# An attention layer on one core: the norm's reciprocal root made from ScalarE's square root and one Newton step, and parts of stage one placed sooner

## The chip, the cores and the metric

One core of a Trainium2 chip runs the whole program. A core has TensorE (PE, matrix products into PSUM banks), VectorE (DVE), ScalarE (ACT), GpSimd (POOL) and SyncE (SP, which here issues DMAs). Each engine takes its instructions strictly from its own list; engines wait for each other by semaphores. The metric is the device time in microseconds (us) of one execution, as a median of runs.

## What is computed

One layer of a bidirectional encoder on 2048 tokens of width 1024: an RMS norm, one projection to q, k, v and a gate, two-dimensional neighbourhood attention with 16 heads of 64, the gate, an output projection with a residual, and a second norm. What the change touches is the first norm and the projection that follows it:

```python
def rmsnorm(x, g):
    xf = x.astype(jnp.float32)
    y = xf * lax.rsqrt(jnp.mean(xf * xf, axis=-1, keepdims=True) + RMS_EPS)
    return (y * g.astype(jnp.float32)).astype(x.dtype)

def neighbourhood_mixer(h, w_in, rpb):
    B, S, _ = h.shape
    proj = h @ w_in
    q, k, v, gate = jnp.split(proj, 4, axis=-1)
    ...
```

## The kernel before

**Chunks and stages.** The 2048 tokens are four chunks of 512. Stage one projects chunks 0 and 1, stage two part of the work for chunks 2 and 3, and the rest of that is fed between the attention's products. float32 operands are split into a high and a low part (`h`, `l`, or `t` and `f` tiles of type F32R), so a product of 128x512 blocks is three matmuls for each of four blocks: twelve matmuls in a row on PE. Products are combined by a seven-product (Strassen-like) scheme over two chunks and two halves of the weights: `P` from 1 to 7, whose operands are the quarters A of the weights or their sums S1 to S4 (`seven.sum`, on DVE), and the quarters B of the inputs or their sums T1 to T4.

**Names.** `form` splits a weight quarter or sum: ACT makes the high part of `f`, DVE the low part. `split` does the same for inputs and gives the tiles `t`, `h`, `l` and `sixths`; `sums4` makes the T4 sums in `spot` and `land` on DVE. `seven.keep` copies a finished bank to `p1`, `acc` (ACT); `add` makes `u` from a bank and that copy (DVE) before a later product goes on in the same bank; `out_` and `evac`/`first_out` write `tmp` from a bank. `tmp` is multiplied by `rb` (on DVE for the first six units, on POOL from unit 6 on) and stored through DRAM tiles `kd`, `qd`, `sgd`. `keep`, `form` and the gate's tanh all stand in ACT's one list.

**Products.** `seq` in `stage_one` lists the products as pairs (unit n, P); `step(i)` issues product i. Positions 0 to 11 are P = 1 and 2 of units 0 to 5. From 12 on they are (0,6), (1,6), (0,7), (0,5), (1,7), (0,4), (1,5), (0,3), (1,4), (1,3), then the same ten for units 2 and 3: product 14 is (0,7), product 17 is (0,4), product 22 is (2,6) and product 24 is (2,7). P = 6, 7 and 4 of a unit share a bank, so product 14 may start only when DVE has taken `u` of product 12 out of it, and product 24 only after `u` of product 22. All other work is attached to a position, either as code between two `step` calls or by `on(i, f, ...)`, which calls `f` after product i. There is no scheduler behind it: the order in which the code issues instructions is the order on each engine.

**The statistics.** The inputs arrive a second time as rows (`load_rows`). `square_rows` squares eight half rows of a chunk on ACT and accumulates the sums. `stats(c)` turns them into a mean square `m` and a reciprocal root `rt`, 128x4 numbers. For chunk 0 the root is fourteen small DVE steps with `m` and `rth` (half of `rt`, by which the values are scaled); for chunks 1, 2 and 3 DVE makes a first guess and POOL three Newton steps of four instructions each. `diagonal(c)` puts `rt` on diagonals `dg` and splits them into `dgh` and `dgl`; `spread_rstd(c)` multiplies these with ones on PE into `prb`, which gives the row `rb[c]` that every output of the chunk is multiplied with. For chunk 1 this pair of matmuls stands behind product 20. Outputs of chunk 1 that were made before are held and scaled by `scale_held`.

**ACT's tables.** ACT's functions lie in tables; the program loads one at its start and another for the square roots of the last norm.

Of the kernel before, what the change touches and what calls it, by code (L numbers as in the profile page):

```python
# [11 lines left out]
F32 = mybir.dt.float32  # L12
F32R = mybir.dt.float32r
BF16 = mybir.dt.bfloat16
I32 = mybir.dt.int32
AF = mybir.ActivationFunctionType
OP = mybir.AluOpType
# [60 lines left out]
def build(ctx, tc, x, xr, xt, wg, bias, w_out, n0, nf, out):  # L78
    nc = tc.nc
# [12 lines left out]
    def pool(name, bufs):  # L92
        p = ctx.enter_context(tc.tile_pool(name=name, bufs=bufs))
        return lambda shape, dt, nm: p.tile(shape, dt, name=nm, tag=name)
# [28 lines left out]
    ev = pool("ev", 8)  # L123
    rbp = pool("rbp", 3)
    tiny = ctx.enter_context(tc.tile_pool(name="tiny", bufs=6))
# [15 lines left out]
    rt = one.tile([128, 16], F32, name="rt")  # L141
    rth = one.tile([128, 8], F32, name="rth")
# [1 line left out]
    accs = [one.tile([128, 512], F32, name=f"acc{i}") for i in range(2)]  # L144
    nc.scalar.dma_start(g0, n0)

    def rsqrt(y, m, n, by=None):
        h = tiny.tile([128, 8], I32, name="h")[:, :n]
        a = tiny.tile([128, 8], F32, name="a")[:, :n]
        nc.vector.tensor_scalar(h, m.bitcast(I32), 1, None, op0=OP.arith_shift_right)  # L150
        nc.vector.tensor_scalar(y.bitcast(I32), h, -1, 0x5F3759DF, op0=OP.mult, op1=OP.add)
        for _ in range(3):
            if by is None:
                nc.vector.tensor_tensor(a, y, y, OP.mult)
                nc.vector.scalar_tensor_tensor(a, a, -0.5, m, op0=OP.mult, op1=OP.mult)
                nc.vector.scalar_tensor_tensor(y, a, 1.5, y, op0=OP.add, op1=OP.mult)
            else:
                by.tensor_tensor(a, y, y, OP.mult)
                by.tensor_tensor(a, a, m, OP.mult)
                by.tensor_scalar(a, a, -0.5, 1.5, op0=OP.mult, op1=OP.add)  # L160
                by.tensor_tensor(y, y, a, OP.mult)

    hh, hl = {}, {}
    rb = {}
# [45 lines left out]
    def square(t, half, tile_):  # L210
        c = t // 4
        if c not in rows:
            rows[c] = tiny.tile([128, 8], F32, name="ss")
        i = 2 * (t % 4) + half
        nc.scalar.activation(tile_, tile_, AF.Square, accum_out=rows[c][:, i:i + 1])

    def stats(c, by=None):
        ss = rows.pop(c)
        m = tiny.tile([128, 8], F32, name="m")[:, :4]
        nc.vector.tensor_tensor(m, ss[:, 0:8:2], ss[:, 1:8:2], OP.add)  # L220
        nc.vector.tensor_scalar(m, m, 1.0 / D, EPS, op0=OP.mult, op1=OP.add)
        rsqrt(rt[:, 4 * c:4 * c + 4], m, 4, by)
        if c < 2:
            (by or nc.vector).tensor_scalar(rth[:, 4 * c:4 * c + 4], rt[:, 4 * c:4 * c + 4], 0.5, None, op0=OP.mult)

    dgs = {}

# [43 lines left out]
    for n, (k, j, ph, c) in enumerate(halves):  # L271
        a = (KINDS[k] + j, ph)
# [259 lines left out]
    def gain(f, k):  # L532
        r = 4 * (int(f[1]) - 1) + k
        return g0[:, r:r + 1]
# [8 lines left out]
    def split_to(h, l, t, scale):  # L543
        if scale is None:
            nc.scalar.activation(h, t, AF.Copy)
            nc.vector.tensor_tensor(l, t, h.bitcast(F32), OP.subtract)
        else:
            nc.scalar.activation(h, t, AF.Copy, scale=scale)
            nc.vector.scalar_tensor_tensor(l, t, scale, h.bitcast(F32), op0=OP.mult, op1=OP.subtract)
# [27 lines left out]
    def place_of(slot_):  # L577
        return slot_[0]([128, slot_[1]], F32R, "t")[:, :512] if isinstance(slot_, tuple) else slot_
# [39 lines left out]
    def stage_one():  # L618
# [16 lines left out]
        def split(f, t, ks, scale=None):  # L635
            for k in ks:
                if f[0] == "T":
                    X1.setdefault(f, []).append(tuple(place_of(a) for a in slots[f][2 * k:2 * k + 2]))
                split_to(*X1[f][k], land[t][k], gain(scale, k) if isinstance(scale, str) else scale)
# [3 lines left out]
        def load_rows(c, hs, p):  # L643
            for h in hs:
                t, j = 4 * c + h // 2, h % 2
                rows_in[t, j] = p([128, 512], F32, "row")
                nc.sync.dma_start(rows_in[t, j], xr[t * 128:t * 128 + 128, 512 * j:512 * j + 512])

        def square_rows(c, hs):
            for h in hs:  # L650
                t, j = 4 * c + h // 2, h % 2
                square(t, j, rows_in.pop((t, j)))
# [35 lines left out]
        E, C = 6, 42  # L688
# [4 lines left out]
        seven = seven_products(us, 0, X1, None)[2]  # L693
        made = [0]

        def forms(to):
            while made[0] <= min(to, len(seq) - 1):
                seven.form(*seq[made[0]])
                made[0] += 1
# [3 lines left out]
        def on(i, f, *a):  # L703
            todo.setdefault(i, []).append((f, a))
# [3 lines left out]
        def step(i):  # L708
            n, P = seq[i]
            seven.product(n, P)  # L710
            now, then[:] = then[:], []
            if i >= 2 * E:
                seven.after(n, P, then)
            elif P == 1:
                seven.keep(n, kp([128, 960], F32, "p1")[:, :512] if n > 3 else accs[n - 2] if n > 1 else None)
            for f in now:
                f()
            for f, a in todo.pop(i, ()):
                f(*a)
# [20 lines left out]
        def sums4(*ks):  # L740
            for k in ks:
                d = land["x21"][k]
                nc.vector.scalar_tensor_tensor(d, d, gain("x21", k), land["x11"][k], op0=OP.mult, op1=OP.subtract)
# [98 lines left out]
        for n in range(2):  # L842
            for f in ("S1", "S2"):
                seven.sum(n, f)
        split("T2", "x11", (1, 2))
        step(7)
        split("T2", "x11", (3,))
        step(8)
        spread_rstd(0)
        forms(12)  # L850
        step(9)
        square_rows(1, range(4))
        load_rows(1, range(4, 8), ev)
        forms(13)
        split("T3", "x22", (0, 1))
        step(10)
        seven.sum(0, "S3")
        forms(14)
        split("T3", "x22", (2, 3))
        step(11)  # L860
        seven.sum(1, "S3")
        first_out(0)
        first_out(1)
        sums4(0)
        forms(15)
        for k in range(4):
            if k < 3:
                on(12 + k, sums4, k + 1)
            on(12 + k, split, "T4", "x21", (k,))
        on(14, square_rows, 1, range(4, 8))  # L870
        on(15, first_out, 2)
        on(16, first_out, 3)
        on(16, stats, 1, nc.gpsimd)
        on(18, diagonal, 1, ev, True)
        on(20, spread_rstd, 1)
        on(21, seven.scale_held)
        on(14, seven.sum, 0, "S4")
        on(16, seven.sum, 1, "S4")

        def ask_pair(a):  # L880
            spot = mkp([128, 3, 512], F32, "raw")
# [25 lines left out]
        for m in range(8):  # L907
            on(C + 5 * m, ask_rows, m)
            on(C + 5 * m + 4, square_more, m)
            if m % 4 == 3:  # L910
                on(C + 5 * m + 4, stats, 2 + m // 4, nc.gpsimd)
        for j in range(4):
            on(C + 9 * j, value_rows, j)
            for d, f in ((3, "S1"), (4, "S3"), (5, "S2"), (6, "S4")):
# [873 lines left out]
    for m in range(cycles + 1):  # L1788
        a = amount[m] - 8
# [89 lines left out]
```

## Time and profile before

| what | value |
|---|---|
| runs: median (lowest to highest of 3) | 1016.49 us (1015.69 to 1017.59) |
| profiled execution: device time | 1016.97 us |
| its span, first to last instruction | 1015.2 us |
| mean granted clock of PE | 0.996 |
| busy: PE, DVE, ACT, POOL | 998.7, 775.3, 511.6, 155.9 us |
| DMA: mean over the span | 225 GB/s |

The profile is of one execution. Its device time is 1.8 us more than its span, which runs from the first to the last instruction. A line number such as L449 is the line of the kernel that issued the instruction, `out<-in` are tile names without their numbers. In a timeline each row has its start, its length, engine, line, operation, tiles, the number of instructions merged into it, and in brackets the idle time of that engine before it with what ended it. Stage one takes the first quarter of the span.

### The profile page before, as it was taken

To read this page: it belongs to the slowest core of one execution; us is meant where nothing else is said; L and a number is where in the kernel's file an instruction comes from. 1 tells how busy PE (TensorE), PEld (TensorE's weight loads), DVE (VectorE), ACT (ScalarE), POOL (GpSimd) and SP (SyncE) were. 2 spreads that over 40 slices of the span, in tenths; PEclk is the share of its full clock that TensorE was granted. 3 is DMA by queue.
4 is the path that set the end of the run, shared out by engine and by line. 5 is a ranking of instruction groups with operands and counts; after the bars stand their busy time and mean duration, and the time that the engine had idled before them with its cause. 6 is when DMAs were issued, how large, how long until landed. Compare 5 with 4: busy or idle time off the path is not lost. (4 is left out here: it accounts for less than half of the span.)

```text
span 1015.2 us, 19596 instructions
## 1 busy us (share of the span) xinstructions
PE 998.7 (98%) x6904; PEld 797.1 (79%) x6904; DVE 775.3 (76%) x1710; ACT 511.6 (50%) x1257; POOL 155.9 (15%) x263
## 2 busy tenths in 40 slices
PE   9999999999999999999999999999999999999997
PEld 6877888878888888888888777777777767777876
DVE  5988888978665876766765676778788888787876
ACT  7863235445335342333434465677767657553443
POOL 0002001242200000000000123243333323221100
PEclk9999999999999999999999999999999999999999
DMA  8934437767957846656565797879987779799553
GB/s 293 351 101 131 152 123 257 242 218 255 353 174 231 270 121 191 208 185 188 196 203 182 221 272 233 267 232 285 282 253 260 202 242 289 224 347 356 138 157 104
DMA packets 150122, 228.19 MB, mean 225 GB/s; under 512 B 13640, under 2 KB 65096, under 8 KB 150024
## 3 DMA queue, kind: packets, MB, share of 16 engines
q1 hardware_dynamic: 148152, 223.92, 68.8%
q0 software_dynamic: 1440, 2.62, 1.7%
q8 instruction: 54, 0.88, 0.3%
q14 instruction: 44, 0.36, 0.1%
q10 hardware_dynamic: 432, 0.40, 0.1%
HBM read 160.83 MB, written 66.06 MB: 223 GB/s over the span
## 5 line engine op out<-in xcount | busy, mean ns | idle before, releaser
L1314 POOL TENSOR_SCALAR x<-x,st 128x360 f32<-128x360 f32 (+5 forms) x192 | 106.5, 571 | 529.1 <-DVE st L1307 528.8
L449 PE MATMUL pp<-h,f 128*128 128x512 f32 x576 | 186.3, 391 | 0.0
L449 PE MATMUL pp<-t,f 128*128 128x512 f32 x702 | 172.0, 390 | 3.0 <-DVE u L462 3.0
L449 PEld LDWEIGHTS pp<-t,f 128*128 128x128 f32 x702 | 131.5, 188 | 31.4 <-ACT f L431 2.9
L1302 ACT ACTIVATE x<-x,st 128x360 f32<-128x360 f32 (+5 forms) x256 | 134.2, 525 | 26.4 <-DVE st L1296 26.4
L449 PEld LDWEIGHTS pp<-h,f 128*128 128x128 f32 x576 | 108.8, 189 | 22.8
L449 PE MATMUL pp<-l,f 128*128 128x512 f32 x288 | 112.5, 391 | 0.0
L1296 DVE CUSTOM_DVE_ANT_0 x<-s,em 128x360 f32<-128x360 f32 (+5 forms) x256 | 102.4, 454 | 1.8 <-PE s L1287 1.4
L432 DVE TENSOR_TENSOR f<-raw,f 128x512 fp32r<-128x512 f32 x105 | 75.8, 727 | 21.3 <-ACT f L431 21.1
L1361 PEld LDWEIGHTS o<-pta,vt 120*64 120x64 f32 (+2 forms) x1024 | 68.7, 137 | 22.7 <-DVE st L1296 15.2
L1361 PE MATMUL o<-pta,vt 120*64 120x192 f32 (+5 forms) x1024 | 83.4, 316 | 0.3 <-issue 0.3
L431 ACT ACTIVATE f<-raw 128x512 fp32r<-128x512 f32 x105 | 63.2, 621 | 40.7 <-DVE raw L438 25.8
L1331 DVE COPY pta<-ph 120x512 f32<-120x512 f32 (+5 forms) x96 | 56.0, 637 | 32.7 <-PE ph L1342 32.5
L1287 PE MATMUL s<-kt,q 64*64 64x360 f32 (+5 forms) x1024 | 78.7, 420 | 1.2 <-DVE y L1437 1.0
L1333 ACT ACTIVATE pta<-ph 120x512 f32<-120x512 f32 (+5 forms) x96 | 46.8, 558 | 62.4 <-PE ph L1342 62.3
L449 PEld LDWEIGHTS pp<-l,f 128*128 128x128 f32 x288 | 54.4, 189 | 11.4
L1287 PEld LDWEIGHTS s<-kt,q 64*64 64x64 f32 x1024 | 41.5, 131 | 23.1 <-ACT pta L1333 6.1
L613 PE MATMUL pv<-wh,t 128*128 128x512 f32 x176 | 56.1, 389 | 0.0
L449 PE MATMUL pp<-sixths,f 128*128 128x512 f32 x198 | 52.7, 389 | 0.0
L1647 PE MATMUL py<-woh,f 128*128 128x512 f32 x160 | 50.9, 390 | 0.9 <-DVE y L1437 0.9
L1342 PEld LDWEIGHTS ph<-ident,x 64*120 64x120 f32 (+2 forms) x1408 | 42.5, 128 | 11.3 <-issue 9.5
L470 POOL TENSOR_TENSOR tmp<-tmp,rb 128x512 f32<-128x512 f32 x18 | 28.5, 1591 | 143.8 <-DVE tmp L467 117.6
(225 smaller groups left out, 1867.6 us busy)
## 6 DMA issues: line engine op xcount, KB each, us to landing
raw<-in_wg_dram SPq DMA_DIRECT2D x124, 256.0 KB, 5.1
row<-in_xr_dram SPq DMA_DIRECT2D x34, 256.0 KB, 5.8
vd<-v SPq DMA_DIRECT2D x32, 256.0 KB, 3.3
sgd<-sg SPq DMA_DIRECT2D x32, 256.0 KB, 5.6
q<-qd SPq DMA_DIRECT2D x32, 256.0 KB, 5.6
sgt<-sgd SPq DMA_DIRECT2D x32, 256.0 KB, 6.8
ogd<-og SPq DMA_DIRECT2D x32, 256.0 KB, 3.4
kt<-kd SPq DMA_DIRECT2D x16, 480.0 KB, 6.8
```

The costliest lines, as they stand in the source:

```text
L431: nc.scalar.activation(t[:, 0], src, AF.Copy)
L432: nc.vector.tensor_tensor(t[:, 1], src, t[:, 0].bitcast(F32), OP.subtract)
L449: nc.tensor.matmul(B[n, P], t[:, int(m == 2), c], x[k][int(m == 1)], start=P in (1, 6, 5) and k == 0 and m == 0, stop=k == 3 and m == 2, s ...
L613: nc.tensor.matmul(p, a[:, o], b, start=P in (1, 6, 5) and k == 0 and m == 0, stop=k == 3 and m == 2, skip_group_check=True)
L1287: nc.tensor.matmul(pst[s][h * 64:h * 64 + 64], qt[a, g * 64:g * 64 + 64], kt[a, :r1 - r0, c0:c0 + 8 * WIDE[C]].rearrange("p r (s c) -> p s ...
L1296: nc.vector.tensor_tensor_reduce(X[i, C][s], pst[s], EM[p, ROW_TYPE[T]][C > 0][s], -1.0, 1e38, OP.add, OP.min, st[:, o:o + 1])
L1302: nc.scalar.activation(X[i, C][s], X[i, C][s], AF.Exp, bias=st[:, o:o + 1], scale=-1.0, accum_out=st[:, 4 + o:5 + o])
L1314: nc.gpsimd.tensor_scalar(X[i, C][s], X[i, C][s], st[:, o:o + 1], 1.0, op0=OP.mult, op1=OP.mult)
L1331: nc.vector.tensor_copy(o, i_)
L1333: nc.scalar.activation(o, i_, AF.Copy)
L1361: nc.tensor.matmul(o[s * 64:s * 64 + 64, g0 * 64:g1 * 64], vt[:k, strip, s * 64:s * 64 + 64], t[:k, n * 64:(n + g1 - g0) * 64], start=stri ...
L1647: nc.tensor.matmul(B[m, P], t[:, a, c], b, start=P in (1, 6, 5) and k == 0 and i == 0, stop=k == 3 and i == 2, skip_group_check=True)
```

## The change

`rsqrt` takes a new form for all four chunks: ACT's square root of `m`, DVE's reciprocal, and one Newton step of three DVE instructions. The halving `rth` for chunk 0 goes from DVE to POOL. In `stage_one` the four row squares 0 to 3 of chunk 1 move from behind product 9 to behind product 7, squares 4 to 7 from 14 to 12, and the loads of rows 4 to 7 go with the former; the S3 sums of units 0 and 1 move from products 10 and 11 to 7, the splits of T3 one product ahead, the T4 sums of blocks 1 to 3 one product ahead, the `first_out` of unit 2 from 15 to 14; statistics, diagonal and spreading of chunk 1 move from products 16, 18 and 20 to 13, 15 and 17, and `scale_held` from 21 to 18.

```diff
--- before.py
+++ after.py
@@ -144,21 +144,13 @@
     accs = [one.tile([128, 512], F32, name=f"acc{i}") for i in range(2)]
     nc.scalar.dma_start(g0, n0)
 
-    def rsqrt(y, m, n, by=None):
-        h = tiny.tile([128, 8], I32, name="h")[:, :n]
-        a = tiny.tile([128, 8], F32, name="a")[:, :n]
-        nc.vector.tensor_scalar(h, m.bitcast(I32), 1, None, op0=OP.arith_shift_right)
-        nc.vector.tensor_scalar(y.bitcast(I32), h, -1, 0x5F3759DF, op0=OP.mult, op1=OP.add)
-        for _ in range(3):
-            if by is None:
-                nc.vector.tensor_tensor(a, y, y, OP.mult)
-                nc.vector.scalar_tensor_tensor(a, a, -0.5, m, op0=OP.mult, op1=OP.mult)
-                nc.vector.scalar_tensor_tensor(y, a, 1.5, y, op0=OP.add, op1=OP.mult)
-            else:
-                by.tensor_tensor(a, y, y, OP.mult)
-                by.tensor_tensor(a, a, m, OP.mult)
-                by.tensor_scalar(a, a, -0.5, 1.5, op0=OP.mult, op1=OP.add)
-                by.tensor_tensor(y, y, a, OP.mult)
+    def rsqrt(y, m):
+        a = tiny.tile([128, 8], F32, name="a")[:, :4]
+        nc.scalar.activation(a, m, AF.Sqrt)
+        nc.vector.reciprocal(y, a)
+        nc.vector.tensor_tensor(a, y, y, OP.mult)
+        nc.vector.scalar_tensor_tensor(a, a, -0.5, m, op0=OP.mult, op1=OP.mult)
+        nc.vector.scalar_tensor_tensor(y, a, 1.5, y, op0=OP.add, op1=OP.mult)
 
     hh, hl = {}, {}
     rb = {}
@@ -214,14 +206,14 @@
         i = 2 * (t % 4) + half
         nc.scalar.activation(tile_, tile_, AF.Square, accum_out=rows[c][:, i:i + 1])
 
-    def stats(c, by=None):
+    def stats(c):
         ss = rows.pop(c)
         m = tiny.tile([128, 8], F32, name="m")[:, :4]
         nc.vector.tensor_tensor(m, ss[:, 0:8:2], ss[:, 1:8:2], OP.add)
         nc.vector.tensor_scalar(m, m, 1.0 / D, EPS, op0=OP.mult, op1=OP.add)
-        rsqrt(rt[:, 4 * c:4 * c + 4], m, 4, by)
+        rsqrt(rt[:, 4 * c:4 * c + 4], m)
         if c < 2:
-            (by or nc.vector).tensor_scalar(rth[:, 4 * c:4 * c + 4], rt[:, 4 * c:4 * c + 4], 0.5, None, op0=OP.mult)
+            nc.gpsimd.tensor_scalar(rth[:, 4 * c:4 * c + 4], rt[:, 4 * c:4 * c + 4], 0.5, None, op0=OP.mult)
 
     dgs = {}
 
@@ -843,39 +835,40 @@
             for f in ("S1", "S2"):
                 seven.sum(n, f)
         split("T2", "x11", (1, 2))
+        square_rows(1, range(2))
         step(7)
         split("T2", "x11", (3,))
+        square_rows(1, range(2, 4))
+        load_rows(1, range(4, 8), ev)
+        for n in range(2):
+            seven.sum(n, "S3")
         step(8)
         spread_rstd(0)
         forms(12)
+        split("T3", "x22", (0, 1))
         step(9)
-        square_rows(1, range(4))
-        load_rows(1, range(4, 8), ev)
         forms(13)
-        split("T3", "x22", (0, 1))
+        split("T3", "x22", (2, 3))
         step(10)
-        seven.sum(0, "S3")
-        forms(14)
-        split("T3", "x22", (2, 3))
-        step(11)
-        seven.sum(1, "S3")
         first_out(0)
         first_out(1)
-        sums4(0)
+        forms(14)
+        step(11)
+        sums4(0, 1)
         forms(15)
         for k in range(4):
-            if k < 3:
-                on(12 + k, sums4, k + 1)
+            if k < 2:
+                on(12 + k, sums4, k + 2)
             on(12 + k, split, "T4", "x21", (k,))
-        on(14, square_rows, 1, range(4, 8))
-        on(15, first_out, 2)
+        on(12, square_rows, 1, range(4, 8))
+        on(14, seven.sum, 0, "S4")
+        on(14, first_out, 2)
+        on(13, stats, 1)
+        on(16, seven.sum, 1, "S4")
         on(16, first_out, 3)
-        on(16, stats, 1, nc.gpsimd)
-        on(18, diagonal, 1, ev, True)
-        on(20, spread_rstd, 1)
-        on(21, seven.scale_held)
-        on(14, seven.sum, 0, "S4")
-        on(16, seven.sum, 1, "S4")
+        on(15, diagonal, 1, ev, True)
+        on(17, spread_rstd, 1)
+        on(18, seven.scale_held)
 
         def ask_pair(a):
             spot = mkp([128, 3, 512], F32, "raw")
@@ -908,7 +901,7 @@
             on(C + 5 * m, ask_rows, m)
             on(C + 5 * m + 4, square_more, m)
             if m % 4 == 3:
-                on(C + 5 * m + 4, stats, 2 + m // 4, nc.gpsimd)
+                on(C + 5 * m + 4, stats, 2 + m // 4)
         for j in range(4):
             on(C + 9 * j, value_rows, j)
             for d, f in ((3, "S1"), (4, "S3"), (5, "S2"), (6, "S4")):
```

Three places in the built order. Past `rsqrt` the line numbers of the changed kernel are eight lower. First ACT, around the copy `p_` of the first of units 4 and 5 (product 8's bank) and the form `f<-s` behind it; `row,ss` are the row squares, `t` and `sixths` splits of inputs. Before:

```order
L431 ACTIVATE f<-raw 128x512 x2
L545 ACTIVATE t<-land 128x512 x4
L457 ACTIVATE p_740<-pp 128x512
L247 ACTIVATE rb<-prb 128x512
L431 ACTIVATE f<-s 128x512
L457 ACTIVATE p_763<-pp 128x512
L215 ACTIVATE row,ss<-row 128x512 x4
L431 ACTIVATE f<-s 128x512
L545 ACTIVATE t<-land 128x512
```

And now:

```order
L423 ACTIVATE f<-raw 128x512 x2
L537 ACTIVATE t<-land 128x512 x3
L207 ACTIVATE row,ss<-row 128x512 x2
L537 ACTIVATE t<-land 128x512
L207 ACTIVATE row,ss<-row 128x512 x2
L449 ACTIVATE p_748<-pp 128x512
L239 ACTIVATE rb<-prb 128x512
L423 ACTIVATE f<-s 128x512
L537 ACTIVATE t<-land 128x512
L537 ACTIVATE sixths<-land 128x512
L449 ACTIVATE p_777<-pp 128x512
L423 ACTIVATE f<-s 128x512
```

The four squares stood between the second copy and the second form; they now stand ahead of the first copy.

The second place is ACT again, at the statistics of chunk 1: `a<-m` is the new square root, `dg` and `dgh` the diagonals. Before:

```order
L545 ACTIVATE t<-spot 128x512
L215 ACTIVATE row,ss<-row 128x512 x4
L431 ACTIVATE f<-s 128x512
L545 ACTIVATE t<-land 128x512
L431 ACTIVATE f<-raw 128x512 x3
L431 ACTIVATE f<-s 128x512
L233 ACTIVATE dg<-ident,rt 128x128 x4
L237 ACTIVATE dgh<-dg 128x512
```

And now:

```order
L537 ACTIVATE t<-spot 128x512
L207 ACTIVATE row,ss<-row 128x512 x4
L423 ACTIVATE f<-raw 128x512
L537 ACTIVATE t<-spot 128x512
L149 ACTIVATE a<-m 128x4
L423 ACTIVATE f<-raw 128x512
L537 ACTIVATE t<-spot 128x512
L423 ACTIVATE f<-s 128x512
L537 ACTIVATE t<-land 128x512
L225 ACTIVATE dg<-ident,rt 128x128 x4
L229 ACTIVATE dgh<-dg 128x512
```

The squares stand ahead of two splits of `spot` that they followed, the root is between forms, and the diagonals come after two forms and two splits from the root. No table load stands at this root; the two others of its kind (chunks 2 and 3) and that of chunk 0 have one ahead.

The third place is PE, at the pair `prb` of chunk 1. Before (the `h` and `l` rows ahead are product 19, the twelve `t` product 20):

```order
L449 MATMUL pp<-l,f 128x512
L449 MATMUL pp<-h,f 128x512
L449 MATMUL pp<-t,f 128x512 x12
L243 MATMUL prb<-dgh,onesr 128x512
L244 MATMUL prb<-dgl,onesr 128x512
```

And now (the first twelve `t` are product 17, the second product 18):

```order
L441 MATMUL pp<-sixths,f 128x512 x9
L441 MATMUL pp<-t,f 128x512 x12
L235 MATMUL prb<-dgh,onesr 128x512
L236 MATMUL prb<-dgl,onesr 128x512
L441 MATMUL pp<-t,f 128x512 x12
```

The pair moved three products ahead; the products themselves keep their order.

## The prediction

> **What bounds the kernel now.** I read the page's busy times first, then the list of what TensorE (PE) waited for, then the timelines of PE, VectorE (DVE), ScalarE (ACT) and GpSimd (POOL) around those waits.
>
> ```profile
> PE 998.7 (98%) x6904; PEld 797.1 (79%) x6904; DVE 775.3 (76%) x1710; ACT 511.6 (50%) x1257; POOL 155.9 (15%) x263
> PE prb L243 <- ACT dgh L237: 1.7, 1, 1.7
> ```
>
> PE is the bound: it is idle 1015.2 - 998.7 = 16.5 us in all. So only what removes a PE wait, or adds one, changes the time. The second row is one of its waits (us, times, longest): once, for `dgh`, the diagonal of the second chunk's statistics; the other pairs `prb` found theirs ready. The next rows are PE's timeline there (start, length, line; the brackets hold the idle time before).
>
> ```profile
> 60.62 5.60 PE L449 MATMUL pp<-t,f 128*128 128x512 f32 x24
> 67.95 0.93 PE L449 MATMUL pp<-t,f 128*128 128x512 f32 x3 [1.72 <-DVE u L462]
> ...
> 88.94 0.49 PE L243 MATMUL prb<-dgh,onesr 128*128 128x512 f32 x1 [1.70 <-ACT dgh L237]
> 89.67 0.80 PE L244 MATMUL prb<-dgl,onesr 128*128 128x512 f32 x1 [0.23 <-DVE dgl L238]
> ...
> 94.28 5.62 PE L449 MATMUL pp<-t,f 128*128 128x512 f32 x24
> 100.26 0.93 PE L449 MATMUL pp<-t,f 128*128 128x512 f32 x3 [0.36 <-DVE u L462]
> ...
> 214.38 0.39 PE L449 MATMUL pp<-h,f 128*128 128x512 f32 x1
> 215.64 0.96 PE L449 MATMUL pp<-t,f 128*128 128x512 f32 x3 [0.87 <-DVE u L462]
> ```
>
> From the first row a matmul starts every (5.60 - 0.39)/23 = 0.2265 us, a product of twelve takes 2.72 us. Lateness is better read from starts than from idle time. The product at 67.95 (position 14) could have started at 60.62 + 5.44 = 66.06. Product 24, at 100.26, lies twelve products and one pair `prb` (2 x 0.24) after 60.62, so without waits at 93.72: PE lost 6.54 us between them. The product at 215.64 could have started at 214.61: 1.03 us lost. The 6.54 holds more than waits:
>
> ```profile
> 66.00:68.00 2.00, 0.28 (x3) 0.08 (x1) 2.00 (x4) 1.15 (x2) 0.00 (x0) 1.00 0.94 271
> ...
> 88.00:90.00 2.00, 0.83 (x2) 0.52 (x3) 1.08 (x2) 1.37 (x3) 0.00 (x0) 0.89 0.00 0
> 90.00:92.00 2.00, 2.00 (x6) 1.52 (x6) 2.00 (x5) 1.64 (x3) 0.00 (x0) 0.50 0.01 4
> 92.00:94.00 2.00, 2.00 (x8) 1.62 (x7) 1.97 (x5) 1.67 (x3) 0.00 (x0) 0.76 0.00 0
> ```
>
> These are windows of 2 us; the third number from the end is the granted clock. After the wait for `prb` it fell to 0.5: (0.22 + 1.00 + 0.48)/0.5 = 3.4 us at half speed, 1.7 us lost. After the equal wait at 66 to 68 it stayed at 1.00.
>
> Why DVE and ACT were late:
>
> ```profile
> 54.80 0.69 DVE L432 TENSOR_TENSOR f<-s,f 128x512 fp32r<-128x512 f32 x1
> 59.04 0.69 DVE L432 TENSOR_TENSOR f<-s,f 128x512 fp32r<-128x512 f32 x1 [3.56 <-ACT f L431]
> ...
> 62.24 0.69 DVE L432 TENSOR_TENSOR f<-raw,f 128x512 fp32r<-128x512 f32 x1 [0.70 <-ACT f L431]
> ...
> 67.11 0.69 DVE L462 TENSOR_TENSOR u<-pp,p 128x512 f32<-128x512 f32 x1
> ...
> 88.92 0.69 DVE L238 TENSOR_TENSOR dgl<-dg,dgh 128x512 fp32r<-128x512 f32 x1 [2.30 <-ACT dgh L237]
> ...
> 99.43 0.69 DVE L462 TENSOR_TENSOR u<-pp,acc 128x512 f32<-128x512 f32 x1
> ```
> ```profile
> 52.14 0.60 ACT L457 ACTIVATE p<-pp 128x512 f32<-128x512 f32 x1 [1.28 <-PE pp L449]
> ...
> 55.45 0.60 ACT L457 ACTIVATE p<-pp 128x512 f32<-128x512 f32 x1 [1.70 <-PE pp L449]
> 55.94 0.62 ACT L215 ACTIVATE row<-row 128x512 f32<-128x512 f32 x1
> ...
> 58.39 0.62 ACT L431 ACTIVATE f<-s 128x512 fp32r<-128x512 f32 x1
> ...
> 86.95 1.28 ACT L233 ACTIVATE dg<-ident,rt 128x128 f32<-128x128 f32 x4 [3.32 <-POOL rt L161]
> ```
>
> DVE stood 3.56 us because ACT did four row squares (55.94 to 58.39, 0.61 each) ahead of the form that DVE wanted. From 59 to 99 it is nearly always busy, so its backlog is what PE meets: `u` at 67.11 releases product 14, `u` at 99.43 releases product 24. It stood again for 2.30 us at `dgl`, whose chain ran through POOL:
>
> ```profile
> 81.05 0.57 POOL L158 TENSOR_TENSOR a<-rt 128x4 f32<-128x4 f32 x1 [79.75 <-DVE rt L151]
> 86.71 0.20 POOL L161 TENSOR_TENSOR rt<-rt,a 128x4 f32<-128x4 f32 x1
> ...
> 206.94 0.57 POOL L158 TENSOR_TENSOR a<-rt 128x4 f32<-128x4 f32 x1 [0.71 <-DVE rt L151]
> 210.64 0.69 DVE L438 TENSOR_TENSOR s<-raw 128x512 f32<-128x512 f32 x1 [1.98 <-DMA raw<-in_wg_dram]
> 210.76 0.63 POOL L161 TENSOR_TENSOR rt<-rt,a 128x4 f32<-128x4 f32 x1
> 211.34 1.73 POOL L470 TENSOR_TENSOR tmp<-tmp,rb 128x512 f32<-128x512 f32 x1
> 213.11 0.63 ACT L381 ACTIVATE tmp<-tmp 128x512 f32<-128x512 f32 x1 [3.15 <-POOL tmp L470]
> 214.29 0.69 DVE L432 TENSOR_TENSOR f<-raw,f 128x512 fp32r<-128x512 f32 x1 [2.36 <-ACT f L431]
> ```
>
> Twelve small POOL steps take 5.9 us for chunk 1 and 4.4 us for chunk 2. The last six rows hold the wait at 215.64: POOL's scaling waits behind the root, ACT behind POOL, DVE behind ACT.
>
> **The change part by part.**
>
> ```profile
> 946.52 1.28 ACT L1459 ACT_TABLE_LOAD   x1
> 947.81 0.20 ACT L1459 ACTIVATE st<-st 128x1 f32<-128x1 f32 x1
> L1307 DVE RECIPROCAL st<-st 128x4 f32<-128x4 f32 x64 | 11.3, 177 | 12.6 <-ACT x L1302 11.7
> 39.17 1.05 ACT L457 ACTIVATE acc<-pp 128x512 f32<-128x512 f32 x2
> ...
> 46.05 0.63 ACT L237 ACTIVATE dgh<-dg 128x512 fp32r<-128x512 f32 x1 [0.86 <-DVE dg L235]
> ```
>
> A root now costs ACT 0.2 us, and DVE four small steps of the reciprocal's kind, about 0.2 us each with the gap behind them. The program has eight table loads where it had two: one ahead of the roots of chunks 0, 2 and 3, one ahead of the next tanh each time; chunk 1 finds chunk 0's table. They are 1.28 us each on ACT. The root starts 947.81 - 946.52 = 1.29 us after the load, so nothing follows the load here. "ScalarE: Activation LUTs", section "What ACT_TABLE_LOAD costs", in the Trainium skill puts a drain of about 1380 ns beside the 1283 ns, 2.66 us for each change of set; the two rows do not show it. By that rule chunk 0's delay below would be 1.4 us longer, product 10 about 0.8 us late, and the gain some 0.8 us smaller.
>
> *Chunk 0's root (about 39 us).* ACT has 1.28 + 0.2 us more, and some 0.1 us of waiting for `m`. Behind it are two copies of PSUM banks, forms 8 and 9, two splits, four value evacuations, `dgh`. The 0.86 us idle before `dgh` take up most, and DVE's shorter root hides the rest but about 0.2 us; the copies (39.17 before) end by 41.8, and PE goes on in the first copied bank only with product 6, which starts 6 x 2.72 + 0.48 us ahead of 60.62, at 43.8. I cost it at 0.2 us of DVE, nothing on PE; without the cover it would be up to 1.5 us.
>
> *Squares 0 to 3 of chunk 1 and the S3 sums earlier.* The four squares (2.45 us) move ahead of the copy at 52.14 into ACT's 1.28 idle us; the copy slips by about 1.3 us to 53.4, done at 54.0, and PE needs it for product 10 at 55.15. The 1.70 us before the second copy cover the rest. The form DVE waited for at 59.04 is ready at about 55, and DVE goes on at 54.8 with the two sums (inputs had landed: S1 was made from them). The 3.56 and 0.70 us go.
>
> ```profile
> 49.41 2.60 SPq L647 DMA_DIRECT2D row<-in_xr_dram  x4
> ...
> DMA to landing us min/median/max: 3.0/3.9/5.7
> ```
>
> The loads of rows 4 to 7 are written two products earlier but keep their place in SP's queue, behind the stores of `v` (first row); they are there long before their squares at 63. The weight loads behind them in that queue (second row: their landing) have one tight case: unit 2's wait for the third split of `spot`, about 72, and DVE wants them at about 79; 5.7 us is the longest landing seen. `u` for product 14 then waits only for PE (63.4) and is done by 64.3: product 14 is not late.
>
> *Statistics of chunk 1 three products earlier, on ACT and DVE.* The 2.30 us at `dgl` go. New waits on DVE: form 16 comes behind a split and four squares on ACT that start when `spot` is done (62.4 + 0.5 + 2.45 + 0.6 = 66.0, DVE free at 65.4: about 0.65 us); the reciprocal waits for the square root (about 0.35 us: step `m` to ACT and back). Queued behind it are form 17 and the next `u`, with 3 us before PE needs them. The second `prb`, now after product 17 (ends 76.9), finds `dgh` at about 73.3 (root done at 70, ACT through its forms and splits at 71.4, then 1.28 + 0.6) and `dgl` at 75.6 (eight large DVE operations of 0.6 after the root): the pair's wait goes, and the half clock with it.
>
> *Sum to product 24.* DVE from 54.80 to 99.43 is 44.63 us, of which idle 3.56 + 0.70 + 2.30 = 6.56, work 38.07. The order up to that `u` holds the same large operations; small ones are two more (0.40); new waits 0.2 + 0.65 + 0.35; some 0.2 for multiplies that now follow their operand at once. 38.07 + 1.80 = 39.87: `u` at 94.67, 4.76 us sooner. PE would be ready at 93.72, so product 24 still waits for DVE, about 1.8 us, longer than before. **4.8 us** is the gain here. Bounds: 6.54 if DVE finds no limit, 3.1 if the new wait costs a half clock of 1.7 us.
>
> *Chunks 2 and 3.* POOL loses its 4.4 us; its scaling can start at about 209.2 once DVE has written `tmp`, although DVE is some 1.1 us later there for the table load and root (the operation at 210.64 stood 1.98 us for a DMA, which hides it). ACT and DVE are then through before PE's 214.61. Gain **1.0 us**; bounds 0 and 1.03. Chunk 3's root has two loads on ACT; its `prb` did not wait, and nothing else there waits on PE: nothing. The scaling of `rth` on POOL for chunk 0 is beside all this.
>
> Sum: 4.76 + 1.03 = 5.8 us. The profiled execution took 1016.97 us (span 1015.2), so 1011.2; the median of the runs is 0.48 lower, 1016.49, which gives **1010.7 us**. PE has next to no idle time after stage one, so what it gains there it keeps.
>
> **The rivals.**
>
> *Half clock (0.15).* The longer wait at product 24 brings another window of half clock. For it: 1.70 + 0.23 us idle did so at 89. Against it: 1.72 us at 66 did not. 1010.7 + 1.7 = 1012.4. "TensorE: Matmul & The Clock Gate" in the Trainium skill, section "Why this matters for your kernels", asks only for no gaps over about 3 us; by that no wait here would do it and this case would fall away. The drop at 89 after 1.93 us speaks against that rule.
>
> *DVE is no limit (0.08).* All 6.54 + 1.03 go: 1016.49 - 7.57 = 1008.9. Against it: DVE's 38 us of work for PE's 33.
>
> *It only moves the waits (0.07).* DVE's new waits for ACT come to the old 6.56: 1016.5. For it: ACT waits for DVE (`spot`, `m`) and DVE for ACT in turn between 61 and 70. Against it: each is one hop, under 0.7 us.
>
> *Table loads on the path (0.10), slower.* Six more loads of 1.28 us stand ahead of forms in ACT's queue; if each reaches PE that is 7.7 us, less 5.8: 1018.4. It decides where ACT's slack is under 1.28 us. For it: DVE takes every form from ACT in order. Against it: forms are made four to six products (11 to 16 us) ahead. With the 2.66 us of the Trainium skill's page "ScalarE: Activation LUTs" it would be 16 us instead of 7.7.
>
> **How the numbers follow.** Forecast 0.60, rivals as above. The range takes forecast, half clock and no limit (0.83): 1008.6 to 1013.4, the ends being those cases with 0.3 and 1.0 us to spare. About 0.2% (2.0 us) can be told from no change: faster 0.83, same 0.07, slower 0.10.
>
> **What would show it.** Right: product 14 without a wait, the second `prb` without one, DVE's stretch to the `u` of product 24 ending near 94 to 95, a wait of 1 to 2 us there, none near 209. Wrong: DVE idle for ACT over 2 us between 55 and 94, a wait for `prb`, a half clock after 90, or PE waits within 10 us of a table load.

## The result, and the profile after

The changed kernel takes 1010.72 us (median of 6 runs, 1009.51 to 1012.34) against 1015.57 us of the kernel before, run beside it (6 runs, 1014.47 to 1017.59); the ratio is 0.9947, 95% interval [0.9937, 0.9958]. A second set gave 1010.76 (5 runs) against 1016.68 (15 runs), 0.9944 [0.9930, 0.9957]. The forecast was 1010.7, faster by 5.8; the medians differ by 4.85 and 5.92 us. The profiled execution after took 1009.61 us, span 1007.8, at a mean granted clock of 0.999 (before: 1016.97, 1015.2, 0.996).

The page's busy times and PE's list of waits, after (us, times, longest):

```profile
PE 996.5 (99%) x6904; PEld 797.1 (79%) x6904; DVE 773.9 (77%) x1708; ACT 519.4 (52%) x1267; POOL 145.9 (14%) x228
PE pp L441 <- DVE u L454: 1.1, 1, 1.1
```

PE's idle time is 11.3 us instead of 16.5. Of the three waits for `u` one is left, and neither matmul of `prb` is in the list. PE's timeline after (start, length; idle time before in brackets):

```profile
60.89 6.28 PE L441 MATMUL pp<-t,f 128*128 128x512 f32 x27
...
77.21 0.40 PE L235 MATMUL prb<-dgh,onesr 128*128 128x512 f32 x1
77.45 0.40 PE L236 MATMUL prb<-dgl,onesr 128*128 128x512 f32 x1
...
88.62 5.60 PE L441 MATMUL pp<-t,f 128*128 128x512 f32 x24
95.31 0.94 PE L441 MATMUL pp<-t,f 128*128 128x512 f32 x3 [1.09 <-DVE u L454]
...
204.23 2.88 PE L441 MATMUL pp<-t,f 128*128 128x512 f32 x12
209.76 0.98 PE L441 MATMUL pp<-t,f 128*128 128x512 f32 x3
```

The 27 matmuls from 60.89 on run through product 14. Product 24 starts at 95.31, 4.95 us sooner than 100.26, and still waits for DVE. The product that started at 215.64 now starts at 209.76. Two products after 204.23 would be 209.67, so it is late by 0.09 us. DVE's and ACT's timelines after, at the steps that the prediction walked through:

```profile
55.35 1.28 DVE L430 TENSOR_TENSOR raw<-raw 128x512 f32<-128x512 f32 x2
58.36 0.68 DVE L424 TENSOR_TENSOR f<-s,f 128x512 fp32r<-128x512 f32 x1
63.89 0.68 DVE L454 TENSOR_TENSOR u<-pp,p 128x512 f32<-128x512 f32 x1
66.38 0.69 DVE L424 TENSOR_TENSOR f<-raw,f 128x512 fp32r<-128x512 f32 x1 [0.55 <-ACT f L423]
69.48 0.18 DVE L150 RECIPROCAL rt<-a 128x4 f32<-128x4 f32 x1 [0.27 <-ACT a L149]
74.97 0.68 DVE L230 TENSOR_TENSOR dgl<-dg,dgh 128x512 fp32r<-128x512 f32 x1
94.48 0.68 DVE L454 TENSOR_TENSOR u<-pp,acc 128x512 f32<-128x512 f32 x1
```
```profile
39.85 1.28 ACT L149 ACT_TABLE_LOAD   x1
41.15 0.20 ACT L149 ACTIVATE a<-m 128x4 f32<-128x4 f32 x1
...
53.71 0.61 ACT L449 ACTIVATE p<-pp 128x512 f32<-128x512 f32 x1
...
72.74 0.63 ACT L229 ACTIVATE dgh<-dg 128x512 fp32r<-128x512 f32 x1
```

Between 55 and 95 us the waits of 3.56, 0.70 and 2.30 us on DVE are gone; 0.55 and 0.27 us have come. `u` of product 24 starts at 94.48 and ends at 95.16, and PE starts behind it.

### The profile page after: what moved, and what is told of

It reads as the page before. It is cut to its first block, busy times and chain, and to the rows that moved or that the text cites. A ratio compares the mean times of both kernels' runs of the same rounds, so it can differ in the third digit from the quotient of the medians.

```text
span 1007.8 us, 19563 instructions
## 1 busy us (share of the span) xinstructions
PE 996.5 (99%) x6904; PEld 797.1 (79%) x6904; DVE 773.9 (77%) x1708; ACT 519.4 (52%) x1267; POOL 145.9 (14%) x228
## 5 line engine op out<-in xcount | busy, mean ns | idle before, releaser
L424 DVE TENSOR_TENSOR f<-raw,f 128x512 fp32r<-128x512 f32 x105 | 75.6, 725 | 20.3 <-ACT f L423 20.2
L441 PEld LDWEIGHTS pp<-l,f 128*128 128x128 f32 x288 | 54.1, 188 | 11.3
L1335 PEld LDWEIGHTS ph<-ident,x 64*120 64x120 f32 (+2 forms) x1408 | 42.5, 128 | 11.3 <-issue 9.5
```

What stands on the lines that cost most here:

```text
L424: nc.vector.tensor_tensor(t[:, 1], src, t[:, 0].bitcast(F32), OP.subtract)
L441: nc.tensor.matmul(B[n, P], t[:, int(m == 2), c], x[k][int(m == 1)], start=P in (1, 6, 5) and k == 0 and m == 0, stop=k == 3 and m == 2, s ...
L1335: nc.tensor.transpose(ph[b, h][:k, o:o + 64], X[2 * m + late_, group[g]][s][q, at:at + k], ident[q, q])
```

## The experiments

All kernels are compared by one distance that the start of the program doesn't touch: from PE's start of product 12 (60.62 before, 60.89 after) to the start of the row of 24 matmuls that stands 8.27 us behind product 24 (108.53 before, 103.59 after). Without any wait it would be fifteen products and one pair `prb`, 15 x 2.718 + 0.48 = 41.25 us. Each distance is of one profiled execution: two of the same kernel differ by 0.44 us (the changed kernel), by 1.56 us (new places alone) and by nothing (two multiplies put off). The medians stem from sets on different chips, so kernels of different sets are compared by the ratio to the kernel before, which ran in each set.

| kernel | distance, us | runs: median (range, n) | ratio to before |
|---|---|---|---|
| before | 47.91 | 1015.57 (1014.47 to 1017.59, 6) | |
| changed; once more | 42.70; 42.26 | 1010.72; 1010.76 | 0.9947 [0.9937, 0.9958]; 0.9944 [0.9930, 0.9957] |
| new root alone | 46.14 | 1014.80 (1012.86 to 1015.49, 11) | 0.9983 [0.9974, 0.9991] |
| new places alone; once more | 44.10; 45.66 | 1014.34 (1011.14 to 1016.90, 12); 1014.09 (1010.88 to 1017.89, 8) | 0.9980 [0.9966, 0.9993]; 0.9973 [0.9960, 0.9986] |
| changed, POOL's root for chunks 2, 3 | 42.26 | 1010.60 (1009.65 to 1012.48, 5) | 0.9948 [0.9935, 0.9961] |
| changed, squares back | 43.60 | 1011.32 (1010.12 to 1013.67, 6) | 0.9953 [0.9939, 0.9966] |
| two loads, no cover | 45.27 | 1013.92 (1011.26 to 1018.12, 10) | 0.9985 [0.9969, 1.0001] |
| two loads, covered | 42.69 | 1010.56 (1009.13 to 1013.26, 6) | 0.9948 [0.9930, 0.9967] |
| `prb` one product sooner | 42.28 | 1008.95 (1008.43 to 1009.39, 4) | 0.9929 [0.9914, 0.9944] |
| `prb` two products sooner | 47.40 | 1014.92 (1012.11 to 1018.40, 10) | 0.9984 [0.9968, 1.0000] |
| two multiplies put off; once more | 41.33; 41.33 | 1010.87 (1010.45 to 1011.61, 5); 1009.06 (1008.86 to 1010.30, 5) | 0.9943 [0.9929, 0.9957]; 0.9929 [0.9917, 0.9942] |

**The two halves of the change.** The first takes the new `rsqrt` and `stats` into the kernel before, the second the new places, with the old root on POOL.

```diff
-        on(16, stats, 1, nc.gpsimd)
+        on(16, stats, 1)
```

> The new root alone, all places as before. Theory (DVE's chain sets product 24): DVE loses the 2.30 us at dgl, keeps the 3.56 and 0.70, and gains about 0.75 us of small steps and of waiting for the root; u of product 24 comes 1.5 us sooner than 99.43, so product 24 starts near 98.7 instead of 100.26, although the waits for prb (1.70 + 0.23) and the half clock behind them go; product 14 still waits 1.7 us; the product at 215.64 gains its 1.0 us on top. Sum -2.6 us. Rival (PE's waits count each by itself): 1.70 + 0.23 + 1.7 of half clock + 1.03 go, -4.7 us. Rival (the table loads cost): five loads more, no gain or a loss.

```diff
-        on(13, stats, 1)
+        on(13, stats, 1, nc.gpsimd)
```

> The new places alone, with the old root (DVE for chunk 0, POOL for 1, 2, 3). Theory: DVE loses the 3.56 and 0.70 us, but POOL's 5.9 us for chunk 1 now end three products sooner in the list with no less to wait for: rt at about 75, dgh at 77, so dgl still stands 2 us on DVE and prb 1 to 1.5 us on PE. u of product 24 about 3.4 us sooner than 99.43, product 24 at about 96.9; nothing changes at 215.64. Sum -3.4 us, or -1.7 if the wait for prb brings a half clock that reaches product 24. Together with the new root alone this is more than both at once, since DVE's 2.30 us go by the root only. Rival (waits count each by themselves): product 14's 1.72 goes and prb's stays, -1.7 us.

The timelines of PE and of DVE, first with the new root alone, then with the new places alone:

```profile
100.35 0.93 PE L441 MATMUL pp<-t,f 128*128 128x512 f32 x3 [1.86 <-DVE u L454]
```
```profile
60.91 0.69 DVE L424 TENSOR_TENSOR f<-s,f 128x512 fp32r<-128x512 f32 x1 [3.98 <-ACT f L423]
```
```profile
96.70 0.94 PE L449 MATMUL pp<-t,f 128*128 128x512 f32 x3 [2.29 <-DVE u L462]
```
```profile
76.34 0.69 DVE L238 TENSOR_TENSOR dgl<-dg,dgh 128x512 fp32r<-128x512 f32 x1 [2.34 <-ACT dgh L237]
```

The distance falls by 1.77 us with the root and by 3.81 with the places, 5.58 in sum and 5.21 with both (expected: 1.5 and 3.4). Each half keeps the DVE wait that the other takes away: 3.98 for the form, 2.34 for `dgh`. What PE saves at `prb` by the root comes back at product 24, where it waits 1.86 us instead of 0.36, so PE's waits don't count each by itself. The wait of 1 to 1.5 us that was expected at `prb` with the new places didn't come.

The medians are another matter. By them the root alone gains 1.9 us (2.6 expected) and the places alone 2.3 (3.4 expected), less than the distances say. The profile of the root alone started product 12 at 62.49, 1.87 us later than before, in code that the edit does not touch; this is taken up with the last experiment. The new places alone took 1011.1 in the profiled execution and 1014.3 in the median, at mean clocks from 0.999 to 0.995. A second profile was taken for that.

> The new places with the old root once more, for a second profiled execution. The first took 1011.15 us with no window of half clock, but ten of its twelve runs took 1013 to 1017 at a mean clock of 0.995 to 0.998. Theory (the wait of 2.3 us at product 24 brings a window of half clock in most executions): an execution at 1013 to 1015 shows granted clock 0.5 for 3.4 us, or 6.8 us, within 10 us behind that wait. Rival (the spread comes from the start or from the last stage): the clock is 1.00 between 90 and 115 in a slow execution too, and the time is lost elsewhere.

This execution took 1017.89 us. PE's timeline and the windows of 2 us (granted clock third from the end):

```profile
98.64 1.11 PE L449 MATMUL pp<-t,f 128*128 128x512 f32 x3 [2.31 <-DVE u L462]
```
```profile
98.00:100.00 2.00, 1.36 (x5) 1.11 (x6) 2.00 (x4) 0.00 (x0) 0.00 (x0) 0.81 0.36 118
100.00:102.00 2.00, 2.00 (x6) 1.62 (x5) 0.89 (x2) 0.63 (x1) 0.00 (x0) 0.50 0.82 280
102.00:104.00 2.00, 2.00 (x9) 1.55 (x9) 0.75 (x2) 0.00 (x0) 0.00 (x0) 0.84 0.94 280
```

The same wait brought no half clock in the first execution and (0.38 + 1.00 + 0.32)/0.5 = 3.4 us of it here; the distance is 1.56 us longer. So the window is a matter of the execution. But it is only part of the 6.7 us by which the two executions differ: product 12 started 1.96 us later here (62.85), another 1.7 us went in a window of half clock at 826 to 830, far from the edit, and PE waited 0.75 us for a form of the last stage, where the first execution did not. The rival that was named, spread from the start and the last stage, holds for these parts. Of the twenty executions of this kernel, the four at a mean clock of 0.999 took 1010.9 to 1012.0 us and the sixteen at 0.995 to 0.998 took 1013.2 to 1017.9, so the spread goes with the clock; where the unprofiled ones lost it is not known.

**Chunks 2 and 3.** POOL's Newton steps are put back for these two (the old root stands beside the new one).

```diff
-                on(C + 5 * m + 4, stats, 2 + m // 4)
+                on(C + 5 * m + 4, stats, 2 + m // 4, nc.gpsimd)
```

> The changed kernel with POOL's old root for chunks 2 and 3 only (their two table loads and those for the next tanh go as well). Theory: the term of 1.0 us returns, product at 209.76 late again by 0.9 to 1.0 us, and nothing else: 1.0 us above the changed kernel, product 24 at 95.3 as there. Rival (table loads cost by themselves): four loads of 1.28 us less, up to 5 us faster than the changed kernel. Rival (POOL's steps in DVE's neighbourhood slow DVE): more than 1.0 us.

Its timelines of PE, POOL and DVE:

```profile
203.83 2.88 PE L461 MATMUL pp<-t,f 128*128 128x512 f32 x12
209.43 0.96 PE L461 MATMUL pp<-t,f 128*128 128x512 f32 x3
```
```profile
201.61 0.57 POOL L166 TENSOR_TENSOR a<-rt 128x4 f32<-128x4 f32 x1 [0.71 <-DVE rt L159]
205.57 1.29 POOL L482 TENSOR_TENSOR tmp<-tmp,rb 128x512 f32<-128x512 f32 x1
```
```profile
206.23 1.18 DVE L450 TENSOR_TENSOR s<-raw 128x512 f32<-128x512 f32 x1 [2.90 <-DMA raw<-in_wg_dram]
```

The product is late by 209.43 - 203.83 - 5.44 = 0.16 us, not 1.03, and the median is that of the changed kernel. The expected 0.9 to 1.0 us did not come. The other profiles that keep the root on POOL show why the size differs. Those with the new places alone are late by 0.28 us (211.35 against 205.63 + 5.44) and, in the second, by 0.61:

```profile
209.15 2.88 PE L449 MATMUL pp<-t,f 128*128 128x512 f32 x12
215.20 0.97 PE L449 MATMUL pp<-t,f 128*128 128x512 f32 x3 [0.45 <-DVE u L462]
```
```profile
210.89 1.74 POOL L470 TENSOR_TENSOR tmp<-tmp,rb 128x512 f32<-128x512 f32 x1
```

| profile | root on POOL to its scaling, us | POOL's scaling, us | product late, us |
|---|---|---|---|
| POOL's root for chunks 2, 3 | 3.96 | 1.29 | 0.16 |
| new places alone | 3.96 | 1.29 | 0.28 |
| new places alone, once more | 3.96 | 1.74 | 0.61 |
| before | 4.40 | 1.73 | 1.03 |

Where root and scaling take POOL longer, the product is later, as the prediction's chain has it; the 0.12 us between the first two rows are not explained. In all ten profiles with ACT's root for these chunks it is late by 0.09 us at most. So the root on POOL does cost PE time there, but 0.16 to 1.03 us by execution, and the prediction took the largest of the four. What comes on top of about 0.2 us lies in how POOL and DVE meet: before, DVE's sum (210.64) ran beside the last root step, which took 0.63 us instead of 0.20, and another DVE operation ran beside the scaling; with the root put back, DVE's sum came after the scaling had begun, and it was the sum that took longer, 1.18 us instead of 0.69.

**The squares.** Row squares 0 to 3 of chunk 1, with the loads, go back; the S3 sums stay early.

```diff
         step(9)
+        square_rows(1, range(4))
+        load_rows(1, range(4, 8), ev)
```

> The changed kernel with the row squares 0 to 3 of chunk 1, and the loads of rows 4 to 7, back behind product 9; the S3 sums stay early. If the squares' place made the 3.56 us, as the prediction had it: DVE idle again about 3.5 us before the second form from s, product 24 late by that, +3.5 us on the changed kernel. If the S3 sums and splits that now stand ahead on DVE would have covered it by themselves: ACT reaches the form at about 58.2, DVE wants it at 58.4, so DVE stands only 0.5 us: +0.5 us, product 24 at 95.8.

DVE's timeline:

```profile
59.17 0.69 DVE L424 TENSOR_TENSOR f<-s,f 128x512 fp32r<-128x512 f32 x1 [0.31 <-ACT f L423]
```

DVE stands 0.31 us, not 3.5; the distance is 0.9 us longer than in the first profile of the changed kernel, 1.3 than in the second. Not all of it is the squares': DVE's `dgl` of chunk 0, ahead of the edit, already came 0.43 us later than in the first profile (47.69 against 47.26). The squares' place is the smaller part, given that the S3 sums are early: with them and a split ahead of the form, DVE has work for most of the 3.56 us. The sums back with the squares early wasn't run, so what the squares would give alone is open.

**The price of a table load.** A tanh and a square root of one column are put in, once where DVE waits for ACT's next form, once (the tanh alone, the root being there) where ACT waits for `m`.

```diff
         on(12, square_rows, 1, range(4, 8))
+        on(12, change, AF.Tanh, AF.Sqrt)
```

> The changed kernel with a tanh and a square root of one column on ACT behind the row squares 4 to 7 of chunk 1, ahead of form 16: two table loads and two small activations more, 2.95 us of ACT, where DVE already stands 0.55 us for that form. Theory (a load costs its 1.28 us and counts where DVE's chain has no cover): DVE stands 3.5 us for form 16, u of product 24 comes 2.95 us later and product 24 starts at 98.3: +2.95 us, or +4.6 with a half clock. If each change of table has also a drain of about 1.4 us (by the Trainium skill's page ScalarE: Activation LUTs, section What ACT_TABLE_LOAD costs, an estimate): +5.7 us. Rival (ACT has slack everywhere): 0.

```diff
+        on(13, change, AF.Tanh)
         on(13, stats, 1)
```

> The changed kernel with a tanh of one column on ACT ahead of chunk 1's root: also two table loads more (for the tanh and for the root), now where ACT stands 2.38 us waiting for DVE's m. Theory: the loads do not need m and run in that wait; ACT is through them at 66.87 + 1.28 + 0.20 + 1.28 = 69.6 instead of 69.24: +0.4 us on DVE and at product 24. With a drain: up to +3. Rival (a table load waits for the operands of its activation): +1.3 us.

The timelines of ACT and of DVE, first without cover, then with it:

```profile
64.80 1.28 ACT L222 ACT_TABLE_LOAD   x1
66.09 0.21 ACT L222 ACTIVATE dum<-dum 128x1 f32<-128x1 f32 x1
66.32 1.28 ACT L222 ACT_TABLE_LOAD   x1
67.61 0.20 ACT L222 ACTIVATE dum<-dum 128x1 f32<-128x1 f32 x1
```
```profile
68.37 0.69 DVE L430 TENSOR_TENSOR f<-raw,f 128x512 fp32r<-128x512 f32 x1 [3.20 <-ACT f L429]
```
```profile
65.70 1.28 ACT L222 ACT_TABLE_LOAD   x1
...
67.22 1.28 ACT L151 ACT_TABLE_LOAD   x1
68.51 0.20 ACT L151 ACTIVATE a<-m 128x4 f32<-128x4 f32 x1
```
```profile
68.75 0.18 DVE L152 RECIPROCAL rt<-a 128x4 f32<-128x4 f32 x1 [0.71 <-ACT a L151]
```

Without cover DVE stands 3.20 us instead of 0.55, and the distance grows by 2.57 us over the first profile of the changed kernel and by 3.01 over the second (2.95 expected): two loads of 1.28 us and their two small activations count nearly in full where DVE's chain has no cover. With cover the second load ran from 67.22, before `m` was written (68.04), and DVE stood 0.44 us longer; the distance is the same as in the first profile and 0.43 us longer than in the second (0.4 expected). Cover also needs room: loads and tanh took ACT 2.81 us, and its wait had been 2.38. The Trainium skill's page "ScalarE: Activation LUTs", section "What ACT_TABLE_LOAD costs", has a drain of some 1380 ns with each change; the trace disagrees: the small tanh starts 1.29 us after the start of its load.

**PE's spare time at product 24.** The pair `prb` of chunk 1 goes behind product 16, then 15.

```diff
-        on(17, spread_rstd, 1)
+        on(16, spread_rstd, 1)
```

> The changed kernel with the second pair prb one product sooner, behind product 16. dgl is done at 75.65, PE arrives at 74.49: PE waits about 1.2 us there. Theory (product 24 is set by DVE, PE has 1.09 us to spare): u of product 24 is not later, the wait at product 24 goes down to 0 to 0.1 us, and the time is +0.1 to +0.2 us. Rival (each PE wait counts): +1.2 us. Rival (half clock after a wait): +1.8 us.

```diff
-        on(17, spread_rstd, 1)
+        on(15, spread_rstd, 1)
```

> The changed kernel with the second pair prb two products sooner, behind product 15. PE arrives at about 71.8, dgl is done at 75.65: PE waits about 3.9 us, the longest gap in stage one. Theory: PE then becomes the bound at product 24, 3.9 - 1.09 = +2.8 us, and if a gap brings half clock, as 1.70 + 0.23 us did in the kernel before, a window of 3.4 us at half speed: +4.5 us. If only a gap of about 2 us in a certain place does so, or none: +2.8 us with a granted clock of 1.00.

PE behind product 16, then behind 15, with windows of the latter:

```profile
74.48 0.40 PE L235 MATMUL prb<-dgh,onesr 128*128 128x512 f32 x1
75.26 0.51 PE L236 MATMUL prb<-dgl,onesr 128*128 128x512 f32 x1 [0.39 <-DVE dgl L230]
```
```profile
73.14 0.50 PE L235 MATMUL prb<-dgh,onesr 128*128 128x512 f32 x1 [1.04 <-ACT dgh L229]
75.44 0.80 PE L236 MATMUL prb<-dgl,onesr 128*128 128x512 f32 x1 [1.79 <-DVE dgl L230]
```
```profile
76.00:78.00 2.00, 2.00 (x6) 1.58 (x5) 1.27 (x2) 1.63 (x3) 0.00 (x0) 0.50 0.50 194
78.00:80.00 2.00, 2.00 (x6) 1.52 (x6) 0.11 (x1) 0.00 (x0) 0.00 (x0) 0.50 0.30 91
```

Behind product 16 PE loses about half a microsecond at `prb` (1.2 expected), product 24 no longer waits, and the distance does not grow (42.28): the wait at product 24 had room for it, as the theory said. The time came out better than the +0.1 to +0.2 us expected: 1008.95, four runs at clocks of 0.999 to 1.000, where the changed kernel's eleven, from other sets, have 0.997 to 0.999. That fewer windows of half clock follow when the wait of about 1 us is gone fits this; no trace shows it. Behind product 15 the distance grows by 4.70 us (4.5 expected with half clock), and the clock is at 0.50 after gaps of 1.04 and 1.79 us. The Trainium skill's page "TensorE: Matmul & The Clock Gate", section "Why this matters for your kernels", asks for no gaps over about 3 us; in this trace two shorter ones, within 3.4 us, were enough.

**The last wait taken away.**

```diff
-            if c0 == 0 and c not in rb:
+            if c0 == 0 and (c not in rb or n == 1 and P in (4, 3)):
...
         on(18, seven.scale_held)
+        on(25, seven.scale_held)
```

> The changed kernel with the multiplies by rb of unit 1's last two outputs (P = 4 and 3) put off to behind product 25, where DVE stands 1.43 us waiting for PE. Theory (DVE's chain sets product 24): u of product 24 comes 1.2 us sooner, at about 93.3, PE's last wait in stage one (1.09 us) goes, product 24 starts at 94.2: -1.1 us on the changed kernel. Rival (the next wait takes its place, at product 26 or where the two multiplies land): 0 to -0.5 us.

> The changed kernel once more, beside the next two on one chip. Theory (its wait of 1.09 us at product 24 lies where PE's clock now and then falls to half for 3.4 us, and the length of stage one's first products varies by up to 1.8 us with the start): median 1010.7, runs from 1009 to 1013, the longer ones at a lower mean clock. A profiled execution with no window of half clock and product 24 34.4 us behind product 12.

> The version with two multiplies put off once more. In its first profiled execution product 24 started 33.2 us behind product 12 instead of 34.4 (the 1.1 us are gained there), but product 12 itself at 62.8 instead of 60.9: PE's first matmuls took twice their time for 4 us, in code that the edit doesn't touch. Theory (the late start is chance): median 1009.0 to 1009.6, 1.1 to 1.7 us below the changed kernel on the same chip. Rival (the edit brings the late start): again 1010.9, the same as the changed kernel.

PE's timeline with the two multiplies put off, first profile:

```profile
6.39 1.05 PE L720 MATMUL pv<-wl,h 128*128 128x512 f32 x2
...
62.76 6.28 PE L441 MATMUL pp<-t,f 128*128 128x512 f32 x27
...
90.50 6.28 PE L441 MATMUL pp<-t,f 128*128 128x512 f32 x27
104.09 5.60 PE L441 MATMUL pp<-t,f 128*128 128x512 f32 x24
```

The 27 matmuls from 90.50 run through product 24 without a wait, and the distance is 41.33, 0.08 us above the unhindered 41.25. In the first set the time did not show it (1010.87, as much as the changed kernel). In the profiled execution of that set PE's first matmuls ran at half their pace (1.05 us for two, 0.62 later) until about 10 us, and product 12 started at 62.76. The kernel's second profile, the one with the new root alone and one of the two with the new places alone show the same. In these four PE had waited 0.58 to 0.64 us at 5.4 us for `wh`, the weights of the next matmuls, in the other ten at most 0.54; whether that wait brings the slow start is not shown. None of the edits touches that code. Both profiles of this version began late and neither of the changed kernel's did, so the traces do not exclude the rival that the edit brings the late start. The medians speak against it: run beside the changed kernel the version took 1009.06 against 1010.76, 1.7 us less. The second profile of the changed kernel has product 24 at 94.55, 33.98 us behind product 12 instead of the expected 34.4, and a window of half clock at 818 to 824, where none was expected.

With the `prb` behind product 16 this is the fastest version here (ratio 0.9929 each); the two weren't run together.

## Why the prediction was right

**Product 14, `prb`, ACT's copies.** As worked out: `u` for product 14 starts at 63.89 (done by 64.3 forecast, 64.57 measured), `dgh` is done at 73.37 (73.3), `dgl` at 75.65 (75.6), and neither product 14 nor the pair waits. The copy `p1` stands at 53.71 (53.4), and no gap opens in PE. Chunk 0's root, with its load, cost PE nothing.

**DVE's chain.** `u` of product 24 came at 94.48 (94.67 forecast). Term by term: the three old waits, 6.56 us, went; the new ones were 0.55 and 0.27 us (0.65 and 0.35 forecast); DVE's `dgl` of chunk 0 came at 47.26 instead of 46.72, 0.54 us later (0.2 forecast for chunk 0's root; in the second profile it came at 46.25); the work from there on grew by 0.25 us (0.6 forecast). That makes 4.95 for 4.76, with errors that nearly cancel. PE would have been ready at 88.62 + 5.44 = 94.06, not 93.72, of which 0.27 us is a later product 12, so the wait there was 1.25 us for about 1.8. That DVE sets this product is shown by the put-off multiplies and by the `prb` behind product 16.

**What was wrong in the working.** First, the 3.56 us were put down to the four squares; with the squares back and the S3 sums early only 0.31 us return. Second, the term for chunk 2 has the right mechanism and too sure a size: the root on POOL cost 0.16, 0.28, 0.61 and 1.03 us in four profiles, and the sum took the 1.03 of the one profile it had. With the smallest the sum would have been 4.9 us; the medians, 4.85 and 5.92 us apart, do not tell 4.9 from 5.8. Third, the sum was made against one execution of 1016.97 us. Its span shrank by 7.4 us; 1.2 us of that came between 911 and 934, where a wait of PE for a form of the last stage (1.0 us) is missing after. That wait comes and goes between executions (0.8 us and none with the new places alone, 0.6 and none with the multiplies put off), so it isn't the change's.

That the median came within 0.02 us of the forecast 1010.7 is luck. The forecast took 5.8 off a median of 1016.49 from three runs; beside the change the kernel before took 1015.57, and in four other sets 1016.2 to 1017.0.

**The rivals.** *Half clock*: it came in no window behind product 24 in the two profiles of the changed kernel, but it did in one of the two with the new places alone, behind 2.3 us. *Table loads on the path*: refuted as a sum (7.7 us), confirmed as a mechanism where no wait covers them (two more cost 2.6 to 3.0 us). *DVE is no limit*: refuted by the 1.09 us that remain. *It only moves the waits*: refuted, 0.82 us of new waits stand against 6.56 of old ones.

## What to carry to other kernels

Where one engine's chain sets a product, a PE wait ahead of it is spare time: price a change by what it takes off that chain, and undo its parts one by one before saying which part did it. A term read from one execution can be several times too large: look at the same place in more than one profile. In this kernel a table load was nearly free where ACT waited long enough to hold it, and cost its 1.28 us where it stood ahead of work that DVE wanted. A wait of 1 to 2 us on PE could cost more than its length here, since a window of half clock followed it in some executions.

## What the runs showed that was not expected

- Half clock behind a wait is a matter of the execution. A wait of 2.3 us was followed by 3.4 us of half clock in one execution of a kernel and by none in another; 1.04 and 1.79 us together were followed by about 6.8 us; a wait of 0.7 to 1.0 us near 820 us, in all fourteen profiles, was followed by a window in two.
- POOL's 128x512 multiply and DVE's operations lengthen each other: DVE's sum 0.69 to 1.18 us, POOL's scaling 1.29 to 1.73.
- A table load does not wait for the operand of its activation: it ran at 67.22 for an `m` that was written at 68.04.
- The first matmuls may run at half pace until 10 us, which moves the whole program by up to 2.7 us (product 12 at 60.2 to 62.9).
